# Two recurrent heads per group of small matmuls, the first weights on one queue, and other buffers: a change to a fused decoder layer

## The chip, the cores and the metric

One core of a Trainium2 chip runs the whole kernel. The metric is device time in microseconds (us) of one execution. The kernel before took 729.4 us as the median of three runs (727.81 to 729.68). One more execution was profiled; it took 726.6 us.

Names used: PE is TensorE (matmuls), PEld its weight loads, DVE is VectorE, ACT is ScalarE, POOL is GpSimd, SP is SyncE, which only issues DMAs here. SBUF is the working memory with 128 partitions, PSUM the memory that matmuls write.

## The reference

One layer of a decoder: 512 positions, model width 1024, everything in float32. Three groups of heads read the same normalised input; their outputs are joined and projected, and a feed-forward network follows.

```
h     = rmsnorm(x, norm_mix)
proj  = h @ w_in          # c_q, c_kv, k_rope, hq, hf, hi, hg, mq
y_mla = mla_group(...)    # 4 heads of causal attention from low-rank q and kv
y_hg  = hgrn2_group(hq, hf, hi, hg, ...)
y_mem = mem_group(mq, rmsnorm(mem), ...)   # 4 heads into 256 memory tokens
x     = x + concat(rmsnorm(y_mla), y_hg, rmsnorm(y_mem)) @ w_out
h2    = rmsnorm(x, norm_ffn)
x     = x + (silu(h2 @ w_gate) * (h2 @ w_up)) @ w_down
```

The recurrent group (hgrn2, four heads of width 128) is what the change is mostly about. With a forget gate f per position and feature, q = silu(hq)/sqrt(128), k = 1 - f, v = hi, the output at t is the sum over s <= t of (sum over features of q[t] k[s] f[s+1]...f[t]) v[s]. It is then normalised per head and gated with silu(hg).

## The kernel before, in words

**Order of the work.** The kernel is not issued in the order in which it is written. A recorder collects every operation, with its reads and writes, a class (0 is most urgent, 2 is filling work) and a price from a formula (`price`, L184). A planner (`run`, L241) then simulates the five engines and writes out one fixed order for each: at each step an engine takes what can start first, and among what is ready the lowest class, then the earliest in the program. Several operations may go to one of two or three engines. Buffers are named by a tag with a fixed count (`BUFS`, L426); an operation that needs a new buffer of a tag is held until one is free, and the planner plans with that. Nearly every instruction is therefore issued on L382; the groups of small matmuls that are recorded as one operation ("tiles") are issued on L379. In the profile a tile is called by its tag: tm<-in_xT is a load of the input into a buffer of tag "tm".

**Matmuls.** A float32 product is made of three fp32r matmuls. Each operand is split into a high part (a cast on ACT: wh, xh, hd, pth, mx) and a low part (a subtraction on DVE: wl, xl, ptl, mx). Products accumulate in PSUM: "mm" (three banks), "at" (three), "tr" (two).

**The start.** Weights of the first query and forget projections of the recurrent heads come in five loads (`EARLY`, L396): two from ACT's queue, three from SP's, between the eight loads of the input. The eight gains of the first norm come in a small load of their own on ACT's queue. Seven matmuls of 128 columns on a tile of ones (`WARM`, L395) run while PE waits. For each of eight chunks ACT makes the scaled high part, DVE the low part, and later the squares for the norm are summed in "td" buffers.

**Recurrent heads.** `hg_in` (L685) projects and gates a head: q, k and the running decay. `hg_levels` (L744) makes the scores of one head without ever dividing by a decay. It goes through sub-block sizes m = 1, 2, 4, ... 128. At each level the scores between the halves of every block of 2m are a matmul of q and k, and then q's upper halves and k's lower halves are multiplied by the decay of the other half (DVE, 256 elements a row each), and the decays are combined in pairs. For m up to 16 the scores lie within 32 x 32 squares of the diagonal: 16 small float32 matmuls (128 rows, 32 columns of weights, 32 moving) give all of them into one PSUM tile, and a predicated copy (DVE) takes those of this level into tile "cc". One more such group comes ahead of the levels, for the diagonal itself. For m = 32 there are 8 pieces, for m = 64 four matmuls of 64 x 64, for m = 128 and the two halves full matmuls. A float32 matmul shows as two instructions, so a group of 16 pieces has 32. The levels of one head keep a "p" buffer for the scores and a "p" buffer for the combined decays; there are two. `hg_out` (L812) multiplies scores with values and normalises, `hg_final` (L822) gates and splits the result into xh and xl.

**Column sums.** `colsum` (L534) sums squares over partitions: 16 small matmuls with a tile of ones, per tile of squares. It serves the norms and the four query heads of each attention, one call a head.

**The rest.** Memory tokens are loaded in four tiles of tag "td", scaled and split into "mx", and their squares summed. Low-rank projections, query and key projections, the causal attention (softmax in "p" buffers), the memory attention, the output projection in two passes (recurrent and causal parts first, in this order, then the memory part) and the feed-forward part follow. Projections that only need the input's split parts (xh, xl) are filling work of class 2.

Of the kernel before, what the change touches and what calls it, by code (L numbers as in the profile page):

```python
# [45 lines left out]
class Recorder:  # L46
# [137 lines left out]
    def price(self, o, outs, ins):  # L184
# [210 lines left out]
WARM = 7  # L395
EARLY = {0: (1, "p", "scalar"), 1: (2, "p", "scalar"), 3: (2, "tc", "sync"), 5: (2, "tc", "sync"), 7: (1, "tc", "sync")}  # L396
# [10 lines left out]
def body(ctx, tc, t):  # L407
# [14 lines left out]
    def nm(p):  # L422
# [5 lines left out]
        "pth": 2, "ptl": 2, "qr": 1, "p": 2, "mx": 8, "cc": 2, "sm": 12, "sd": 8, "mm": 3, "at": 3, "tr": 2,  # L428
# [27 lines left out]


# [7 lines left out]
    with rec.first(0):  # L465
        A.dma_start(out=sm[:, 0:8], in_=t["sm"][:, 0:8])
# [67 lines left out]
    def colsum(sq, nblk):  # L534

        o = ps_ts()
        T.tiles(o[:, 0:2 * nblk], lhsT=sq, rhs=ones, parts=[
            (o[g:g + 32, 2 * b:2 * b + 2], sq[:, b * P + g:b * P + g + 32], ones, b == 0, b == nblk - 1)
            for b in range(nblk) for g in range(0, P, 32)
        ])  # L540
        return o[:, 0:2 * nblk].rearrange("p (b two) -> p b two", two=2)[:, :, 0]
# [26 lines left out]
    def heads(ap):  # L568
        return ap.rearrange("p (h d) -> p h d", d=P)


    with rec.first(0):
# [3 lines left out]
        early = ([], [])  # L576
        for k in range(KD):
            if k in EARLY:
                n, tag, q = EARLY[k]
                w = sb(tag)[:, :2 * n * P]  # L580
                getattr(rec, q).dma_start(out=w, in_=t["we"][:, 2 * k * P:2 * (k + n) * P])
                pc = piece(w, 0, 2 * n * P)
# [6 lines left out]
            split(r, hi, lo, smc("g_mix", k))  # L589
# [154 lines left out]
    def hg_levels(q, k_, tot):  # L744
        A_ = sb("p", (P, NB, P))
        tt = sb("p")
        C = sb("cc", (P, NB, 32))
        toff = 0

        def scores():  # L750

            o = ps_at()[:, 0:NB * 32].rearrange("p (b t) -> p b t", t=32)
            T.tiles(o, lhsT=k_, rhs=q, parts=[
                (o[g:g + 32, b], k_[:, b * P + g:b * P + g + 32], q[:, b * P + g:b * P + g + 32], b == 0, b == NB - 1)
                for b in range(NB) for g in range(0, P, 32)
            ])
            return o

        o = scores()
        V.tensor_tensor(C, o, eye.unsqueeze(1).broadcast_to([P, NB, 32]), ALU.mult)  # L760
        G.memset(A_, 0.0)
        V.tensor_tensor(q, q, tot, ALU.mult)
        m = 1
        while m <= 128:
            if m <= 16:
                o = scores()
                V.copy_predicated(C, lmask[:, LEVELS.index(m), :].unsqueeze(1).broadcast_to([P, NB, 32]), o)
                if m == 16:
                    for g in range(0, P, 32):
                        A.copy(A_[g:g + 32, :, g:g + 32], C[g:g + 32])  # L770
            elif m == 32:
                o = heads(ps_at())[:, :, :32]
                T.tiles(o, lhsT=k_, rhs=q, parts=[
                    (o[i:i + 32, b], k_[:, b * P + i:b * P + i + 32], q[:, b * P + i + 32:b * P + i + 64], b == 0, b == NB - 1)
                    for b in range(NB) for i in (0, 64)
                ])
                for i in (0, 64):
                    A.copy(A_[i:i + 32, :, i + 32:i + 64], o[i:i + 32])
            elif m == 64:
                o = heads(ps_at())[:64, :, :64]  # L780
                for b in range(NB):
                    T.matmul(o[:, b], lhsT=k_[:, b * P:b * P + 64], rhs=q[:, b * P + 64:(b + 1) * P], start=b == 0, stop=b == NB - 1, skip_group_check=True)
                A.copy(A_[:64, :, 64:], o)
            else:
                pts = [new_pt(2), new_pt(4)]
                for g, pt in enumerate(pts):
                    for x in pt:
                        G.memset(f(x)[:, 4 * g + 2, :], 0.0)
                o = ps_at()
                for i, s in enumerate((0, 2)):  # L790
                    T.matmul(o[:, i * P:(i + 1) * P], lhsT=k_[:, s * P:(s + 1) * P], rhs=q[:, (s + 1) * P:(s + 2) * P], start=i == 0, stop=i == 1, skip_group_check=True)
                for i in range(2):
                    split(o[:, i * P:(i + 1) * P], pts[i][0][:, 4 * i + 1, :], pts[i][1][:, 4 * i + 1, :])
            n = S // (2 * m)
            tv = tot.rearrange("p (n two) -> p n two", two=2)
# [661 lines left out]
```

## Time and profile before

| | before |
|---|---|
| median of three runs | 729.4 us (727.81 to 729.68) |
| profiled execution | 726.6 us |
| its span, first to last instruction | 724.7 us |
| PE busy | 704.3 us (97%) |
| DVE busy | 563.0 us (78%) |
| ACT busy | 382.6 us (53%) |
| groups' instructions in the recurrent heads (at<-tm,tm on L379) | 832 |

The page and the views give, for a group of instructions, out<-in by the program's tags, shapes, the count, busy time, the mean of one in ns, and the idle time of the engine before them with what ended it. "Busy" of PE counts pipelined matmuls from their start to a modelled end, so two matmuls in a row overlap: the distance between two starts is what a matmul costs PE.

### The profile page before, as it was taken

The page shows a single profiled execution, that of the slowest core. Times are in us where ns is not written, and L with a number is a line of the kernel's source. Part 1 is how long each engine was busy: PE and PEld are TensorE (multiplying, and loading weights), DVE is VectorE, ACT ScalarE, POOL GpSimd, SP SyncE. Part 2 cuts the span into 40 slices and gives each one's busy share as a digit, 9 for nine tenths or more (in the row PEclk, how much of TensorE's full clock was granted, in tenths as well). Part 3 has the DMA queues.
Part 4 walks back from the last instruction along what each step waited for, and adds up shares of the span by engine and source line. Part 5 has one row for each costly group of instructions (what it writes and reads, how often), then busy time and mean ns, then how long its engine had stood idle before and what let it go on. Part 6 is the DMA issues. An engine that isn't in the chain of part 4 may idle for free.

```text
span 724.7 us, 13261 instructions
## 1 busy us (share of the span) xinstructions
PE 704.3 (97%) x4808; PEld 584.5 (81%) x4808; DVE 563.0 (78%) x1326; ACT 382.6 (53%) x726; POOL 93.0 (13%) x129
## 2 busy tenths in 40 slices
PE   7999999799999999899999999999999999999997
PEld 6888777678788887688686888888888899999886
DVE  6888889869988799897899979947548677538742
ACT  6743443437684487556477674635543355543420
POOL 0000000000000000000223323213202303410000
PEclk9999999999999999999999999999999999999999
DMA  8232122014621142121999999968958757942241
GB/s 277 76 107 70 60 89 74 24 38 140 195 97 34 55 137 92 49 59 44 263 266 214 256 215 226 229 151 220 219 146 165 180 135 172 219 110 41 66 131 72
DMA packets 47873, 98.07 MB, mean 135 GB/s; under 512 B 5568, under 2 KB 15680, under 8 KB 47808
## 3 DMA queue, kind: packets, MB, share of 16 engines
q1 hardware_dynamic: 33552, 73.75, 31.3%
q0 software_dynamic: 13824, 23.07, 20.3%
q8 instruction: 38, 0.62, 0.3%
q10 hardware_dynamic: 432, 0.40, 0.2%
q14 instruction: 27, 0.22, 0.1%
HBM read 95.11 MB, written 2.10 MB: 134 GB/s over the span
## 4 chain that ended last, share of the span: by engine, by line
PE 90%; DVE 6%; ACT 2%; issue 1%; DMA 0%; DVEq 0%; ACTq 0%
PE mm L382 47%; PE tr L382 21%; PE at L382 20%; PE at L379 1%; DVE wl L382 1%; PE tr L379 1%; DVE ptl L382 1%; DVE hd L382 1%; ACT L382 1%; DVE y L382 1%; DVE sm L382 0%; ACT p L382 0%; DMA tm<-in_xT 0%; DVE tm L382 0%; DVE tc L382 0%
## 5 line engine op out<-in xcount | busy, mean ns | idle before, releaser
L382 ACT CAST wh<-wr 128x512 fp32r<-128x512 f32 (+2 forms) x136 | 80.8, 598 | 113.7 <-PE mm L382 64.9
L382 DVE TENSOR_TENSOR wl<-wr,wh 128x512 fp32r<-128x512 f32 (+2 forms) x148 | 96.5, 657 | 33.2 <-issue 11.4
L382 PE MATMUL mm<-xh,wh 128*128 128x512 f32 x248 | 99.4, 406 | 5.5 <-ACT wh L382 3.2
L382 PE MATMUL mm<-xh,wl 128*128 128x512 f32 x248 | 100.2, 405 | 0.0
L382 PE MATMUL mm<-xl,wh 128*128 128x512 f32 x248 | 99.9, 404 | 0.2 <-DVE xl L382 0.2
L382 DVE TENSOR_TENSOR wl<-y,wh 128x512 fp32r<-128x512 f32 (+1 forms) x84 | 53.1, 637 | 42.2 <-PE tr L382 17.3
L382 ACT CAST wh<-y 128x512 fp32r<-128x512 f32 (+1 forms) x83 | 48.2, 582 | 66.5 <-PE at L382 34.2
L382 DVE TENSOR_TENSOR wl<-mx,wh 128x512 fp32r<-128x512 f32 (+1 forms) x72 | 45.6, 642 | 27.6 <-PE tr L382 14.8
L382 PE MATMUL mm<-wh,hd 128*128 128x512 f32 (+2 forms) x188 | 64.0, 366 | 0.7 <-ACT wh L382 0.7
L382 ACT CAST wh<-mx 128x512 fp32r<-128x512 f32 (+1 forms) x65 | 37.8, 584 | 40.9 <-PE at L382 22.1
L382 PEld LDWEIGHTS mm<-xh,wh 128*128 128x128 f32 x248 | 47.1, 191 | 14.5 <-ACT wh L382 3.6
L382 PEld LDWEIGHTS mm<-xl,wh 128*128 128x128 f32 x248 | 47.5, 191 | 8.7 <-DVE xl L382 0.7
L382 PEld LDWEIGHTS mm<-xh,wl 128*128 128x128 f32 x248 | 47.2, 190 | 8.4
L382 PE MATMUL at<-wh,hd 128*128 128x512 f32 (+1 forms) x132 | 49.7, 377 | 0.0
L382 POOL DMA_DIRECT2D y<-in_wu x36 | 32.5, 943 | 96.9 <-DVE wl L382 80.7
L382 PE MATMUL tr<-xl,wh 128*128 128x512 f32 x112 | 43.8, 391 | 0.0
L382 PE MATMUL tr<-xh,wl 128*128 128x512 f32 x112 | 43.7, 390 | 0.0
L382 PE MATMUL tr<-xh,wh 128*128 128x512 f32 x112 | 43.7, 390 | 0.0
L382 PEld LDWEIGHTS mm<-wh,hd 128*128 128x128 f32 x188 | 34.6, 188 | 5.8 <-ACT wh L382 1.1
L382 PE MATMUL mm<-wl,hd 128*128 128x512 f32 (+2 forms) x100 | 37.0, 370 | 0.2 <-DVE wl L382 0.2
L382 POOL MEMSET p<- 128x128 f32 (+1 forms) x12 | 3.7, 312 | 258.1 <-PE tr L382 116.8
L382 PE MATMUL mm<-wh,v 128*128 128x512 f32 (+1 forms) x96 | 36.1, 376 | 0.6 <-ACT v L382 0.6
(371 smaller groups left out, 1750.5 us busy)
## 6 DMA issues: line engine op xcount, KB each, us to landing
wr<-in_wf SPq DMA_DIRECT2D x19, 512.0 KB, 3.4
wr<-in_wd SPq DMA_DIRECT2D x16, 512.0 KB, 5.2
mx<-in_wg SPq DMA_DIRECT2D x24, 256.0 KB, 5.6
mx<-in_wu SPq DMA_DIRECT2D x24, 256.0 KB, 4.8
y<-in_wu POOLq DMA_DIRECT2D x24, 256.0 KB, 6.0
tm<-in_xT SPq DMA_DIRECT2D x16, 256.0 KB, 3.6
wr<-in_wt SPq DMA_DIRECT2D x8, 512.0 KB, 4.1
wr<-in_wo SPq DMA_DIRECT2D x8, 512.0 KB, 3.5
```

The source lines that it names most:

```text
L379: r = self.nc.tensor.matmul(get(a), lhsT=get(b), rhs=get(c), start=first, stop=last, skip_group_check=True)
L382: r = getattr(getattr(self.nc, o.eng), o.name)(*[get(a) for a in o.args], **{k: get(a) for k, a in o.kw.items()})
```

## The change

- `hg_levels` takes a list of two heads and goes through the levels with both. A group of small matmuls holds the pieces of both heads: 64 instructions at m = 2 to 16, 32 at m = 32, 16 of 64 x 64. The group for the diagonal and the one for m = 1 become one with 128, for which q times its decay goes to a new buffer of tag "y". One DVE operation then takes the scores of both heads. The combined decays are written in place, so the second "p" buffer holds the other head's scores. The level m = 128 moves into `hg_out`.
- `colsums` sums two tiles of squares in one group, for the query heads of both attentions.
- The five first weight loads are all on ACT's queue, ahead of everything else; the first also brings the eight gains. The constant pi/2 is made on ACT, right behind them, instead of on DVE. The warm-up is 12 matmuls of 512 columns.
- Homes: memory tokens load into "y" instead of "td"; the recurrent heads' split outputs go to "mx" instead of xh and xl, and those of the causal attention to xh and xl instead of "mx".
- The planner's price of a group of small matmuls has another formula.

```
-                return 180 + 64 * len(o.kw["parts"]) / len({self._rng(p[0])[2] for p in o.kw["parts"]})
+                return 310 + 1.81 * sum(max(35, self._free(p[2])) for p in o.kw["parts"]) / len({self._rng(p[0])[2] for p in o.kw["parts"]})
...
-WARM = 7
-EARLY = {0: (1, "p", "scalar"), 1: (2, "p", "scalar"), 3: (2, "tc", "sync"), 5: (2, "tc", "sync"), 7: (1, "tc", "sync")}
+WARM = 12
+EARLY = {0: (1, "p"), 1: (2, "p"), 3: (2, "tc"), 5: (2, "tc"), 7: (1, "tc")}
...
-        "pth": 2, "ptl": 2, "qr": 1, "p": 2, "mx": 8, "cc": 2, "sm": 12, "sd": 8, "mm": 3, "at": 3, "tr": 2,
+        "pth": 2, "ptl": 2, "qr": 1, "p": 2, "mx": 8, "cc": 1, "sm": 12, "sd": 8, "mm": 3, "at": 3, "tr": 2,
...
-    with rec.first(0):
-        A.dma_start(out=sm[:, 0:8], in_=t["sm"][:, 0:8])
...
-            T.matmul(o[:, 0:P], lhsT=ones_r, rhs=ones_r, start=True, stop=True)
+            T.matmul(heads(o), lhsT=ones_r, rhs=ones_r.unsqueeze(1).broadcast_to([P, NB, P]), start=True, stop=True)
...
-    V.memset(hpi, float(np.pi / 2))
...
+    def colsums(sqs, nblk=NB):
+        o = ps_ts()[:, 0:2 * nblk * len(sqs)]
+        ks = [(i, b) for i in range(len(sqs)) for b in range(nblk)]
+        v = o.rearrange("p (i b two) -> p i b two", two=2, b=nblk)
+        T.tiles(o, ones, *sqs, parts=[
+            (v[g:g + 32, i, b], sqs[i][:, b * P + g:b * P + g + 32], ones, (i, b) == ks[0], (i, b) == ks[-1])
+            for i, b in ks for g in range(0, P, 32)
         ])
+        return v[..., 0]
...
+        for k, (n, tag) in EARLY.items():
+            w = ws[k] = sb(tag)[:, :2 * n * P + 8 * (k == 0)]
+            A.dma_start(out=w, in_=t["we"][:, 2 * k * P + 8 * (k > 0):2 * (k + n) * P + 8])
+        gain = ws[0][:, 2 * P:]
+
+        A.mul(hpi, ones[:, 0:1], float(np.pi / 2))
...
-            split(r, hi, lo, smc("g_mix", k))
+            split(r, hi, lo, gain[:, k:k + 1])
...
-    def hg_levels(q, k_, tot):
+    def hg_levels(hs):
+
+        N2 = range(len(hs))
+        As = [sb("p", (P, NB, P)) for i in N2]
+        C = sb("cc", (P, len(hs), NB, 32))
+        old, hs = hs, [(sb("y"), k_, tot) for q, k_, tot in hs]
...
+            T.tiles(o, *[x for i, h in all_ for x in h[:2]], parts=[
+                (o[g:g + 32, i, b], h[1][:, b * P + g:b * P + g + 32], h[0][:, b * P + g:b * P + g + 32], (i, b) == (all_[0][0], 0), (i, b) == (all_[-1][0], NB - 1))
+                for i, h in all_ for b, g in ps_
             ])
...
+        def put(o, m):
+            V.copy_predicated(C, lmask[:, LEVELS.index(m), :].unsqueeze(1).unsqueeze(1).broadcast_to([P, len(hs), NB, 32]), o)
+
+        for (q, _, tot), (q1, _, _) in zip(old, hs):
+            V.tensor_tensor(q1, q, tot, ALU.mult)
...
+            if m == 1:
+                o, o1 = scores([old, hs])
+                V.tensor_tensor(C, o, eye.unsqueeze(1).unsqueeze(1).broadcast_to([P, len(hs), NB, 32]), ALU.mult)
+                put(o1, 1)
+            elif m <= 16:
+                put(scores([hs])[0], m)
...
+            hs = [(q, k_, step_up(q, k_, tot, m)) for q, k_, tot in hs]
             m *= 2
+        return [(A_,) + h for A_, h in zip(As, hs)]
...
+        if m < 128:
+            V.tensor_tensor(tot[:, 0:n], tv[:, :, 0], tv[:, :, 1], ALU.mult)
+        return tot
...
-        hi = sb("xh", dt=F32R)
-        lo = sb("xl", dt=F32R)
+        hi = sb("mx", dt=F32R)
+        lo = sb("mx", dt=F32R)
         split(y, hi, lo)
         mix[4 + h] = (hi, lo)
...
+    for h, st in enumerate(hg_levels(qkf)):
+        yh.append(hg_out(h, *st))
+    qkf = [hg_in(2), hg_in(3)]
+    for h, st in enumerate(hg_levels(qkf)):
+        yh.append(hg_out(2 + h, *st))
...
-            r = sb("td", (P, 2, NM))
+            r = sb("y", (P, 2, NM))
             DMA.dma_start(out=r, in_=t["memT"][:, k * S:(k + 1) * S].rearrange("p (a b) -> p a b", a=2))
...
+            sq.append(sumsq([o]))
+        if h % 2:
+            V.tensor_copy(sq_n[:, :, h - 1:h + 1].rearrange("p b h -> p h b"), colsums(sq[-2:]))
...
-    group_norm(ym, 0, "g_mla", ("mx", "mx"))
+    group_norm(ym, 0, "g_mla", ("xh", "xl"))
```

More of the change, by code (lines that the diff above doesn't have):

```diff
@@ L534, in colsum @@
     def colsum(sq, nblk):
[L536 to L539, printed above, removed]
+        return colsums([sq], nblk)[:, 0]
+    def colsums(sqs, nblk=NB):
[5 more added lines that the diff above has]
+            for i, b in ks for g in range(0, P, 32)
         ])
-        return o[:, 0:2 * nblk].rearrange("p (b two) -> p b two", two=2)[:, :, 0]
+        return v[..., 0]
     def spread(r):
@@ L777, in hg_levels @@
[L777 to L783, printed above, removed]
-            else:
[L785 to L793, printed above, removed]
@@ new lines, in hg_out @@
+    def hg_out(h, A_, q, k_, tot):
+        pts = [new_pt(2), new_pt(4)]
+        for g, pt in enumerate(pts):
+            for x in pt:
+                G.memset(f(x)[:, 4 * g + 2, :], 0.0)
+        o = ps_at()
+        for i, s in enumerate((0, 2)):
+            T.matmul(o[:, i * P:(i + 1) * P], lhsT=k_[:, s * P:(s + 1) * P], rhs=q[:, (s + 1) * P:(s + 2) * P], start=i == 0, stop=i == 1, skip_group_check=True)
+        for i in range(2):
+            split(o[:, i * P:(i + 1) * P], pts[i][0][:, 4 * i + 1, :], pts[i][1][:, 4 * i + 1, :])
+        step_up(q, k_, tot, 128)
@@ L918, in body @@
     w = [piece(r, 0, 512) for r in wuq]
+    sq = []
     for h in range(4):
```

97 lines of the change are left out of this document (44 added, 53 removed).

## Prediction

> **What bounds the kernel now.** I read the page first: the engines' shares and the chain that ended last.
>
> ```profile
> span 724.7 us, 13261 instructions
> ...
> PE 704.3 (97%) x4808; PEld 584.5 (81%) x4808; DVE 563.0 (78%) x1326; ACT 382.6 (53%) x726; POOL 93.0 (13%) x129
> ...
> PE 90%; DVE 6%; ACT 2%; issue 1%; DMA 0%; DVEq 0%; ACTq 0%
> ```
>
> PE is busy for 97% of the span and is 90% of the chain. An edit pays only if it takes time out of PE's own stream or fills one of PE's few holes. The view of windows (window, length, then PE, PEld, DVE, ACT and POOL busy, granted clock, DMA share, GB/s) shows the holes around the recurrent heads and the attention behind them.
>
> ```profile
> 34.00:127.00 93.00, 92.58 (x1303) 75.73 (x1303) 80.86 (x250) 39.32 (x80) 3.32 (x12) 1.00 0.25 79
> 127.00:138.00 11.00, 7.06 (x135) 4.80 (x132) 9.07 (x23) 5.33 (x12) 0.00 (x0) 0.84 0.12 37
> 138.00:201.00 63.00, 62.59 (x500) 50.30 (x498) 53.72 (x177) 36.59 (x73) 0.20 (x1) 1.00 0.34 110
> 201.00:275.00 74.00, 74.00 (x525) 61.59 (x524) 63.70 (x167) 46.76 (x95) 1.81 (x7) 1.00 0.26 82
> 275.00:298.00 23.00, 18.94 (x126) 14.95 (x124) 19.71 (x52) 13.63 (x28) 0.20 (x1) 0.93 0.22 69
> ```
>
> PE is full from 34 to 127 and from 138 to 275 us. DVE stands next behind it, at 87% and 85% of the two stretches before 201. The holes are 127 to 138 (3.9 us idle, granted clock 0.84) and 275 to 298 (4.1 us idle, at the end of the causal attention). So up to about 275 us PE's time is what a saving is counted in.
>
> **Fewer groups of small matmuls.** PE's own order of time around one group of score pieces (start, duration), then the row that groups all of them (count, busy us, mean ns of one, idle before):
>
> ```profile
> 93.85 0.40 PE L382 MATMUL mm<-xh,wl 128*128 128x512 f32 x1
> 94.17 0.46 PE L379 MATMUL at<-tm,tm 128*32 128x32 f32 x32
> 94.56 0.50 PE L382 MATMUL mm<-xh,wh 128*128 128x512 f32 x1
> 94.90 0.40 PE L382 MATMUL mm<-xl,wh 128*128 128x512 f32 x1
> 95.13 0.39 PE L382 MATMUL mm<-xh,wl 128*128 128x512 f32 x1
> ```
>
> ```profile
> L379 PE MATMUL at<-tm,tm 128*32 128x32 f32 x832 | 13.0, 199 | 2.9 <-DVE tm L382 2.9
> ```
>
> Two large matmuls in a row start 0.23 us apart (94.90 to 95.13). From 93.85 to 94.90 there are two of these and one group: 1.05 - 2 x 0.23 = 0.59 us for the group. Inside the group, from the first small start to the last, lie 0.46 - 0.20 = 0.26 us (its busy time less the mean of one); those are the 32 instructions of its 16 pieces. The other 0.33 us is a fixed price, paid at the two ends where PE goes from large to small and back. Merging two groups saves 0.33 us and keeps the 0.26.
>
> How many fixed prices go: the 832 instructions are 24 groups of 32 (six a head) and 4 groups of 16. With two heads together a pair has one group for the first two score sets, four for sub-blocks 2 to 16, and one for 32: six, twelve in all instead of 28. The 64-wide step goes from four groups to two; I give it the same price. That is 18 prices x 0.33 = 5.9 us. The query projections' column sums, groups of 16 pieces too and priced alike, go twice from four to two. The first two groups saved lie before 201, where PE is full: 2 x 0.33 = 0.6 us. The other two stand under the causal attention, whose own end leaves PE idle at 275 to 298; I count them at nothing (0.6 us if that hole were gone).
>
> The bounds: nothing, if all of the 0.59 went with the number of small matmuls, and 18 x 0.59 = 10.6 us, if a second head's pieces came free. The small starts 8 ns apart exclude the first, and the 0.26 us excludes the second.
>
> The Trainium skill speaks against the saving: "TensorEngine Tiling (Array Packing)", section Performance Considerations, gives about 60 cycles to each matmul, which I estimate at 25 ns with the 2.4 GHz of "TensorE: Matmul & The Clock Gate". Taken one after the other, 32 of them would be 0.8 us with nothing fixed, merging would save nothing, and the sum below would be 4.0 instead of 10.5. The trace disagrees: 32 starts lie in 0.26 us.
>
> On DVE the pairing halves a number of instructions too:
>
> ```profile
> L382 DVE COPY_PREDICATED cc<-lmask,at 128x128 f32<-128x128 uint8 x20 | 5.9, 297 | 2.0 <-PE at L379 2.0
> ...
> L382 DVE TENSOR_TENSOR tm<-tm,p 128x256 f32<-128x256 f32 x56 | 22.4, 417 | 0.0
> ```
>
> 20 x 0.297 becomes 10 of twice the width, priced like the 256-wide row at 0.42: 5.9 to 4.2, so 1.7 us less of DVE. The scaling of the queries, now into a buffer of its own, is the same work. The running product written in place waits for the two multiplications before it, on the same engine, in order.
>
> **The new wait: two heads in step.** A merged group waits for the later of two heads, and on PE the large matmuls queued behind it wait too. What covers it is other ready work; which order results is the planner's. In its favour: no head now holds a "p" buffer from its first level for running products, so the second pair need not wait for the first pair's scores to be read out. DVE, at 87%, is the engine that could make PE wait. Bounds: 2 us gained (its 1.7 saved) to 3 us lost. I take 1.0 us lost.
>
> **The hole at 127 us.** PE's order of time there, then the timing of tile td:
>
> ```profile
> 127.53 0.46 PE L379 MATMUL at<-tm,tm 128*32 128x32 f32 x32
> 130.40 0.46 PE L379 MATMUL at<-tm,tm 128*32 128x32 f32 x32 [2.41 <-DVE tm L382]
> 131.94 0.50 PE L382 MATMUL mm<-xh,wh 128*128 128x512 f32 x1 [1.08 <-ACT td L382]
> ...
> 133.68 0.80 PE L382 MATMUL mm<-xh,wl 128*128 128x512 f32 x1
> ...
> 135.98 0.63 PE L382 MATMUL mm<-xl,wh 128*128 128x512 f32 x1
> ```
>
> ```profile
> L382 SPq DMA_DIRECT2D td<-in_memT x4: 327/328/423, 95.4 to 123.5; - x4
> ...
> L382 ACT ACTIVATE td<-mm x3: 597/597/597, 131.3 to 134.7; 128x512 f32<-128x512 f32 x3
> ```
>
> At 127.5 PE has only one head's levels left and waits 2.41 us for DVE's step of them. It has no large matmul to put between, because the next projection waits for ACT's square of an earlier one (td<-mm, 131.3 us), which has to read the PSUM bank before it comes free. That square waits for one of three td buffers, and these are held by the memory tokens (td<-in_memT, the last at 123.5 us) and their sum. In the change the tokens load into y, so td is free and the square can run when the projection ends. The hole costs 11.0 - 7.06 = 3.9 us idle, and five matmuls from 133.68 to 135.98 take 2.30 us where 5 x 0.23 = 1.15 is usual: together 5.1 us. I take 4.0 of it; bounds 0 (another buffer is next) and 5.1.
>
> On the half rate the Trainium skill ("TensorE: Matmul & The Clock Gate", Part 1, the table of states) says that the clock falls after an idle window of about 3.4 us. Here the longest idle was 2.41 us and the clock fell. By that rule the hole would cost 3.9 us, and the term would be about 3.1.
>
> **The start.** Two stretches of PE's windows (warm-up, first real matmuls), and the rows of ACT and PE that lead to the second:
>
> ```profile
> 1.20:3.10 1.90, 1.76 (x7) 1.57 (x7) 0.00 (x0) 0.00 (x0) 0.10 (x1) 1.00 0.58 135
> ...
> 6.10:10.45 4.35, 4.31 (x10) 3.32 (x11) 3.93 (x7) 3.64 (x7) 0.53 (x1) 1.00 1.04 375
> ```
>
> ```profile
> 3.78 1.28 ACT L382 ACT_TABLE_LOAD   x1 [3.78 <-DMA tm<-in_xT]
> ...
> 6.14 1.22 PE L382 MATMUL mm<-xh,wh 128*128 128x512 f32 x2 [3.17 <-ACT wh L382]
> ```
>
> PE's first 10 real matmuls take 4.31 us, where 10 x 0.23 = 2.3 would do: as if it had started at full rate at 8.1 (6.1 + 2.0). Twelve warm-up matmuls of 512 columns instead of seven of 128 keep PE busy up to them: 12 x 0.43 (half rate, 4.31/10) = 5.2 us from 1.2 to 6.4 at most, less if the rate rises on the way. I expect the real ones at full rate then.
>
> Against it stands ACT's queue, which now issues five weight loads before its first arithmetic. SP's queue at the start, its wait, and the time to landing of a first weight load show what that meets:
>
> ```profile
> 0.74 1.33 SPq L382 DMA_DIRECT2D tm<-in_xT  x3
> 2.12 0.43 SPq L382 DMA_DIRECT2D tc<-in_we  x1
> 2.59 1.64 SPq L382 DMA_DIRECT2D tm<-in_xT  x2
> ```
>
> ```profile
> SPq L382 <- DMA smv<-in_sm: 0.9, 1, 0.9
> ```
>
> ```profile
> p<-in_we ACTq DMA_DIRECT2D x1, 128.0 KB, 3.7
> ```
>
> With ACT's three loads SP's fifth is the eighth of all. Its sixth, the ninth, waits 0.9 us until the first of all, the gain vector from ACT's queue, has landed, at 2.59 + 0.43 + 0.9 = 3.9. So eight are in flight at a time. In the change loads alternate between the two queues, and the ninth is ACT's fifth. It waits for the first weight load, which lands at 0.74 + 3.7 = 4.4, or at 3.9 if it is as quick as the gain vector was. Behind this wait are queued the issue (0.43), the table load (1.28), the one-column constant (I take 0.2, under the 0.297 of a 128-wide DVE row above) and the two splits (PE started 1.08 us after the table load's end): 6.9 to 7.4. I take 7.1 at full rate: 8.1 - 7.1 = 1.0 us gained. Bounds: 2.5 (no wait: five issues end at about 3.0, the table load at 4.3, the first split starts when its data is there at 4.4, PE at 5.6) and -1.0 (PE at 7.1 and cold again, worth 2.0). DVE's clearing of that constant goes, at nothing.
>
> **Homes without a price.** The splits of the recurrent heads' outputs move from xh, xl to mx, and the causal attention's from mx to xh, xl. The former can run earlier (mx is free after the memory projections), the latter need the input's split halves read out by the last gate projection. PE's idle time at 275 to 298 says that no such projection was left by then, so they are free before the attention ends. If that cover went, the output projection would start on the recurrent heads' part, which is first in its order. I count 0.
>
> **The sum.** 5.9 + 0.6 + 4.0 + 1.0 - 1.0 = 10.5 us. The profiled execution took 726.6 us (span 724.7 and 1.9 around it), so 716.1. It lies 2.8 under the median of the runs, 729.4, so the median goes to 718.9, forecast 719.
>
> **The rivals.** Savings turn to idle: the causal attention's chain, not PE, ends at 298, and if it starts no earlier, PE only runs out of other work sooner. Against it: PE is full for 63 us before it, with a chain that feeds on PE's own projections. Only start and noise would be left, a gain of 0 to 2: about 728.5, no change.
>
> Paired squares hold td: the first head's squares now stay in one of the three td buffers until the second head's projection is squared, while gates want two more. This is the same shortage as at 127 us, and it decides where a bank's square has to wait while PE has no other ready work. A hole of 5.1 us each: two give back 10.2 of the 10.5 (729, no change), three (two in the query projections, one in the memory queries) give 10.5 - 15.3 = -4.8: 734, slower. Against it: paired projections follow one another, and with little else in td.
>
> The hole at 275 goes too: the recurrent heads' outputs leave y and are ready sooner, and the memory attention, which needs y, fills in. Its 4.1 us more give 715.
>
> The loads do not do what they are moved for: ACT is held as above and PE is cold, -1.0 instead of 1.0: 721, inside the forecast's own range of 715 to 725.
>
> The price goes with the count: 0.59 us over 32 instructions is 18 ns each, nothing is fixed, and merging saves neither the 5.9 nor the 0.6: a gain of 4.0, 725.4. Against it: the starts 8 ns apart. This is what the rule on the cost of each matmul in the Trainium skill ("TensorEngine Tiling (Array Packing)", Performance Considerations) would do here.
>
> **How the numbers follow.** Forecast 0.61, the better case 0.15, idle instead of gain 0.12, td slower 0.09, a price by count 0.03. A difference under 0.3% (2.2 us) can't be told from none. Faster is 0.61 + 0.15 + 0.03 and 0.01 of the idle case, 0.80; same 0.11; slower 0.09. The range, 712 to 729, takes in all cases but the slower one, and the largest saving of the start and the hole (1.5 + 1.1 more than taken, with the better case).
>
> **What would show it.** L379's score instructions stay 832 in 12 clusters of 32, 64 and 128, each a fixed 0.33 us; no PE wait of 1 us or more for ACT td near 120 us; PE at 0.23 us spacing from its first real matmul, at about 7 us; PE's time from 34 to 201 shorter by some 9 us. Wrong, if that stretch keeps its length with PE idle in it, or the clusters cost 1.2 us for two heads.

## The result and the profile after

The change took the median from 729.08 us (727.81 to 729.68) to 712.05 us (711.61 to 712.68): 0.9769 of before, 95% interval 0.9752 to 0.9786, 17.0 us less. The profiled execution took 712.43 us. The first lines of the page after answer to those of before:

```profile
span 710.7 us, 13219 instructions
...
PE 698.4 (98%) x4813; PEld 582.9 (82%) x4813; DVE 558.4 (79%) x1305; ACT 384.2 (54%) x731; POOL 94.0 (13%) x129
...
PE 93%; DVE 4%; ACT 2%; DMA 1%; issue 0%; DVEq 0%; ACTq 0%
```

PE is busy for 5.9 us less, of a span that is 14.0 us shorter; the other 8 us were idle time. The windows show where. The stretches answer roughly to those of before, the later ones 8 to 14 us earlier (window, length, PE, PEld, DVE, ACT, POOL, granted clock, DMA share, GB/s):

```profile
34.00:118.00 84.00, 83.66 (x1225) 71.70 (x1224) 72.90 (x201) 41.46 (x82) 2.05 (x7) 1.00 0.27 89
118.00:130.00 12.00, 11.68 (x169) 9.08 (x170) 10.61 (x41) 5.29 (x14) 0.00 (x0) 1.00 0.12 36
130.00:190.00 60.00, 59.73 (x541) 48.68 (x541) 55.31 (x186) 37.42 (x78) 0.71 (x4) 1.00 0.36 115
190.00:262.00 72.00, 72.00 (x518) 60.12 (x517) 63.20 (x171) 42.58 (x90) 2.39 (x8) 1.00 0.25 78
262.00:284.00 22.00, 20.19 (x137) 15.79 (x136) 21.11 (x53) 14.87 (x28) 1.19 (x2) 1.00 0.31 96
```

The hole of 127 to 138 us is closed: 0.3 us idle in 12, at a granted clock of 1.00 instead of 0.84. The hole at the end of the causal attention is 1.8 us instead of 4.1, also at full clock. From the view of PE's waits (total, times, longest):

```profile
PE mm L382 <- ACT xh L382: 4.8, 3, 2.2
...
PE mm L379 <- DVE td L382: 0.6, 2, 0.3
```

The three for ACT's xh are the start (1.3), the attention's end (1.2) and the end of the memory attention (2.2). None is left for ACT's td.

**Which part came where.** For a finer measure I counted PE's large matmuls at the distance of their starts when PE is full (0.227 us for 512 columns, 0.173 for 384, 0.147 for 320, 0.120 for 256; some 625 us in all) and compared the times at which two kernels have done the same amount. "Lead" is how much earlier than in the shown profile of before that is, at six of its times:

| kernel | 15 us | 118 | 201 | 302 | 360 | 700 | last block of third head | third head |
|---|---|---|---|---|---|---|---|---|
| before | 0 | 0 | 0 | 0 | 0 | 0 | 4.89 | 25.4 |
| after | -0.6 | 5.7 | 10.4 | 14.8 | 12.2 | 14.1 | 2.85 | 20.2 |
| e12 before again | -0.9 | -1.0 | -1.3 | -2.0 | -1.9 | -1.9 | | |
| e1 homes old | -0.3 | 6.0 | 10.7 | 15.2 | 13.4 | 13.8 | 2.85 | 20.2 |
| e2 tokens in td | -0.2 | 5.0 | 2.9 | 1.7 | -3.0 | -1.6 | 4.89 | 24.3 |
| e3 before, tokens in y | 0.2 | -2.7 | 2.1 | 0.9 | 1.0 | 0.8 | 4.89 | 25.4 |
| e4 one head a group | -0.2 | -0.8 | 4.6 | 4.6 | -0.8 | 0.4 | 4.89 | 24.3 |
| e5 table load early | -0.7 | 5.7 | 10.5 | 15.0 | 13.1 | 13.8 | 2.85 | 20.2 |
| e6 old warm-up | -0.7 | 5.8 | 10.5 | 15.0 | 12.9 | 14.8 | 2.85 | 20.2 |
| e7 single sums | -0.2 | 6.2 | 10.1 | 9.1 | 9.1 | 8.8 | 6.07 | 24.0 |
| e8 old price | 0.0 | 7.1 | 11.6 | 12.1 | 7.6 | 9.1 | 4.91 | 24.4 |
| e9 before, tanh | -0.5 | -0.5 | -0.8 | 1.6 | 0.2 | -0.3 | 4.36 | 22.8 |
| e10 after, tanh | -0.3 | 6.0 | 10.6 | 16.0 | 16.4 | 15.0 | 2.83 | 20.0 |
| e11 e8 with tanh | -0.3 | 6.8 | 11.2 | 11.2 | 11.3 | 11.2 | 4.36 | 22.6 |

The last two columns belong to the end of the causal attention: the time from the exponential of the third query block to that of the last one in its third head, and the length of that head, from the end of the second head's last value matmul to the end of its own. The fourth head, not in the table, takes 22.8 us in before and 24.1 in after, so the two heads together are 3.9 us shorter and not 5.2. The shown execution of before lies some 2 us below its median, so a lead reads that much smaller than a difference of medians.

So after has lost 0.6 us at 15 us, gained 10.4 by 201, 4.4 more by 302 at the attention's end, lost 2.6 of it by 360 and got 1.9 back.

**A merged group.** PE's order of time around one group of two heads in after (start, duration), and the rows of all groups of score pieces:

```profile
44.06 0.31 PE L382 MATMUL mm<-wl,xh 128*128 128x320 f32 x1
44.30 0.76 PE L379 MATMUL at<-y,tm 128*32 128x32 f32 x64
44.99 0.41 PE L382 MATMUL mm<-wh,xl 128*128 128x320 f32 x1
45.24 0.31 PE L382 MATMUL mm<-wh,xh 128*128 128x320 f32 x1
45.39 0.31 PE L382 MATMUL mm<-wl,xh 128*128 128x320 f32 x1
```

```profile
L379 PE MATMUL at<-y,tm 128*32 128x32 f32 x704 | 9.5, 199 | 0.0
...
L379 PE MATMUL at<-y,tm 128*64 128x64 f32 x32 | 2.5, 226 | 0.1
...
L379 PE MATMUL at<-tm,tm 128*32 128x32 f32 x128 | 1.9, 198 | 0.0
```

From 44.06 to 45.24 there are two matmuls of 320 columns (45.39 - 45.24 = 0.15 each) and one group of 64: 1.18 - 0.30 = 0.88 us. Inside it, 0.76 - 0.20 = 0.56. The fixed part is 0.32, as it was 0.33 around 32 instructions. The score instructions are 704 + 128 = 832, as before. Their distance depends on how many groups of 32 columns the pieces go to in turn: at m = 2 to 16 it is four groups, and 64 instructions lie in 0.56 us (9 ns apart); at m = 32 it is two, and the 32 instructions at 62.57 us last 0.70 us, 0.50 from the first start to the last (16 ns apart). So each column group takes some 32 to 36 ns a matmul in both, an estimate from these two rows.

**The start.** ACT (its queue's issues are ACTq) and PE in after:

```profile
0.74 0.89 ACTq L382 DMA_DIRECT2D p<-in_we  x2
1.66 3.21 ACTq L382 DMA_DIRECT2D tc<-in_we  x3
4.90 1.28 ACT L382 ACT_TABLE_LOAD   x1 [4.90 <-DMA p<-in_we]
```

```profile
1.22 4.84 PE L382 MATMUL tr<-ones_r 128*128 128x512 f32 x12 [1.22 <-DVE ones_r L382]
7.37 0.73 PE L382 MATMUL mm<-xh,wh 128*128 128x512 f32 x2 [1.31 <-ACT xh L382]
...
8.49 0.40 PE L382 MATMUL mm<-xh,wl 128*128 128x512 f32 x1
8.73 0.39 PE L382 MATMUL mm<-xl,wh 128*128 128x512 f32 x1
```

The fifth load holds ACT until 4.87, the table load follows, and PE starts at 7.37 at full rate (8.49 to 8.73). All of this is as forecast, and yet the lead at 15 us is -0.6. At full rate PE has to wait for the splits: its weight loads wait 0.49, 0.43 and 0.54 us for DVE's low part (xl) at 8.15, 9.81 and 12.94 us, while ACT works on without a wait. From 7.37 to 15 us PE loses 1.4 us that way, counted as the distance of its starts above 0.227 us; in before it lost 2.1 to the half rate from its start at 6.14 on.

### The profile page after: what moved, and what is told of

The parts are those of the page before. It is cut to its first block, busy times and chain, and to the rows that moved or that the text cites. A ratio compares the mean times of both kernels' runs of the same rounds, so it can differ in the third digit from the quotient of the medians.

```text
span 710.7 us, 13219 instructions
## 1 busy us (share of the span) xinstructions
PE 698.4 (98%) x4813; PEld 582.9 (82%) x4813; DVE 558.4 (79%) x1305; ACT 384.2 (54%) x731; POOL 94.0 (13%) x129
## 4 chain that ended last, share of the span: by engine, by line
PE 93%; DVE 4%; ACT 2%; DMA 1%; issue 0%; DVEq 0%; ACTq 0%
PE mm L382 49%; PE tr L382 21%; PE at L382 21%; PE at L379 1%; PE tr L379 1%; DVE wl L382 1%; DMA p<-in_we 1%; DVE ptl L382 0%; DVE y L382 0%; DVE xl L382 0%; ACT L382 0%; DVE td L382 0%; PE mm L379 0%; DVE qr L382 0%; ACT wh L382 0%
## 5 line engine op out<-in xcount | busy, mean ns | idle before, releaser
L382 DVE TENSOR_TENSOR wl<-wr,wh 128x512 fp32r<-128x512 f32 (+2 forms) x148 | 96.8, 659 | 33.2 <-PE mm L382 11.6
L382 PE MATMUL mm<-xh,wh 128*128 128x512 f32 x248 | 97.4, 398 | 4.8 <-ACT xh L382 4.8
L382 ACT CAST wh<-y 128x512 fp32r<-128x512 f32 (+1 forms) x83 | 48.2, 582 | 68.5 <-PE at L382 35.5
L382 PEld LDWEIGHTS mm<-xh,wh 128*128 128x128 f32 x248 | 46.6, 189 | 13.8 <-ACT xh L382 5.7
L382 PEld LDWEIGHTS mm<-xl,wh 128*128 128x128 f32 x248 | 47.1, 190 | 11.2 <-DVE xl L382 2.5
L382 PE MATMUL at<-wh,v 128*128 128x512 f32 (+1 forms) x96 | 35.9, 374 | 0.0
```

The lines of the kernel that those rows point to most:

```text
L382: r = getattr(getattr(self.nc, o.eng), o.name)(*[get(a) for a in o.args], **{k: get(a) for k, a in o.kw.items()})
```

## The experiments

The medians of before beside the experiments were 728.69 (e1 to e4; 726.56 to 730.87), 728.24 (e5 to e8) and 728.52 us (e9 to e12). The first theory was the prediction's, term by term; its rival was that the tokens' and outputs' homes make up what it counted too small. Later runs asked what decides the attention's end.

**e1_homes_old** (after, only the homes of the outputs back):

```
-        hi = sb("mx", dt=F32R)
-        lo = sb("mx", dt=F32R)
+        hi = sb("xh", dt=F32R)
+        lo = sb("xl", dt=F32R)
...
-    group_norm(ym, 0, "g_mla", ("xh", "xl"))
+    group_norm(ym, 0, "g_mla", ("mx", "mx"))
```

> The changed kernel with the two old homes for the split outputs: recurrent heads in xh and xl, causal attention in mx. The changed kernel left 2.3 us of stalls around the end of the causal attention where before had 5.7, and gained 4.5 us there on the same PE work. Theory H: the new homes did it, since the recurrent heads' outputs no longer wait for the input's split halves to be read; then this run loses 3 to 5 us against the changed kernel (715 to 717) and shows the hole at the end of the causal attention again. Theory P: the attention's chain itself ended earlier against PE's other work, for other reasons; then this run stays within 1.5 us of the changed kernel (711 to 713.5).

Measured: 712.88 us (712.69 to 715.05), ratio 0.9795 [0.9777, 0.9813], at most a microsecond from after. The third head still takes 20.2 us, and the lead at 302 is 15.2. These homes are worth nothing that can be told, and are not what closed the hole at the attention's end.

**e2_tokens_td** (after, memory tokens loaded into td again; shown) and **e3_before_tokens_y** (before, with the opposite edit alone, y for td):

```
-            r = sb("y", (P, 2, NM))
+            r = sb("td", (P, 2, NM))
```

> The changed kernel with the memory tokens loaded into td again. Theory T (the hole at 127 us came from td buffers held by the tokens): a PE wait for a square into td or a hole of 1 us or more comes back between 95 and 145 us, and the time rises by 2 to 5 us (714 to 717). Rival: pairing the heads removed the hole, by ending the recurrent part sooner; then nothing comes back and the time stays within 1.5 us (711 to 713.5).

> The kernel before with one edit: memory tokens load into y instead of td. Theory T: the hole at 127 to 138 us closes, 4 to 5 us faster than before (724 to 725). Rival (pairing removed the hole): heads still go one after another, the hole stays, within 1.5 us of before (728 to 730).

e2: 727.82 us (726.73 to 728.31), ratio 0.999 [0.998, 0.9999]: 15.8 us slower than after. Its window and PE's order of time at the place of the hole:

```profile
118.00:130.00 12.00, 7.02 (x132) 5.49 (x119) 10.75 (x33) 5.66 (x13) 0.00 (x0) 0.72 0.10 36
```

```profile
117.67 0.76 PE L379 MATMUL at<-y,tm 128*32 128x32 f32 x64
122.08 1.30 PE L379 MATMUL at<-y,tm 128*32 128x32 f32 x32 [3.64 <-DVE tm L382]
124.70 0.79 PE L382 MATMUL mm<-xh,wh 128*128 128x512 f32 x1 [1.32 <-ACT td L382]
```

The same two waits as in before, on DVE's step and on ACT's square in td, each longer (3.64 for 2.41, 1.32 for 1.08); I read the difference so that both heads of the pair now stand at this step and neither has other levels to offer. At 201 us 7.5 us are missing (2.9 for 10.4); 5.6 more go at the attention's end and 2.6 after it, most of them at the end of the memory attention.

e3: 725.84 us (725.58 to 727.74), ratio 0.997 [0.996, 0.998], 2.9 us faster than before. The hole at 127 closes: its lead rises by 4.8 us from 118 to 201. But it had lost 2.7 before that, most of it near 26 us, where PE now waits for the first norm's spread:

```profile
27.56 0.62 PE L382 MATMUL tr<-cst,rx 128*128 128x128 f32 x4 [0.82 <-issue]
28.86 0.42 PE L382 MATMUL tr<-wh,xh 128*128 128x320 f32 x1 [0.68 <-ACT RX L382]
```

So the tokens' home is shown to be the hole's cause, alone and with the pairing, and the pairing needs it: the tokens' home is worth 4.8 us at this place in before and 7.5 in after.

**e4_one_head** (after, groups of one head; the first two score sets and the query sums stay merged):

```
-    for h, st in enumerate(hg_levels(qkf)):
-        yh.append(hg_out(h, *st))
+    for h in range(2):
+        yh.append(hg_out(h, *hg_levels(qkf[h:h + 1])[0]))
```

and the same for heads 2 and 3.

> The changed kernel with the levels of one head at a time (the group for the diagonal and the one for m = 1 stay one): 24 groups of score pieces instead of 12 and four 64-wide steps instead of two, 14 fixed prices of 0.33 us more. Theory T (the fixed price is PE's and PE is the bound): 4.6 us slower than the changed kernel, 716 to 717.5. Rival (the price goes with the number of small matmuls): no difference, 711 to 713. Rival (two heads in step cost PE more than they save): faster than 711.

Measured: 726.22 us (724.98 to 727.49), ratio 0.9968 [0.9955, 0.998], 14 us slower than after. Of these only 5.8 lie in the recurrent heads' own stretch (4.6 for 10.4 at 201): 14 more groups at 0.41 us each, for the 4.6 us expected at 0.33. PE's waits between 15 and 195 us are 0.6 longer (1.2 for 0.6), which is half of the difference. The other 8 come later, 4.4 at the attention's end and most of the rest at the end of the memory attention.

**e7_sums_single** (after, each head's column sums by themselves; the cut is the memory attention's, the causal one's is alike):

```
-            if h % 2:
-                V.tensor_copy(vq[:, :, h - 1:h + 1].rearrange("p b h -> p h b"), colsums(sq[-2:]))
+            V.tensor_copy(vq[:, :, h], colsum(sq[-1], NB))
```

> The changed kernel with column sums of the query heads one head at a time again, both attentions: four groups more. Theory: two fixed prices of 0.33 us ahead of the causal attention, 0.7 us slower, and two under it that may cost nothing: 712.5 to 713.4. Rival (pairs of squares hold td buffers): no slower or faster, 710 to 712.

Measured: 717.64 us (717.35 to 718.64), ratio 0.9849 [0.9828, 0.987], 5.6 us slower than after. At 201 us only 0.3 of it is there. By 302 us 5.4 more are lost: the third head takes 24.0 us. The edit's own part there is two more groups, which lie under the second and third heads (205 to 235 us) and cost 0.7 us at the price above; the rest comes from the order.

**e8_price_old** (after, with the planner's old price of small matmuls; the computation is the same, but the planner's order differs, and with it the engine of some casts, copies and scalings):

```
-                return 310 + 1.81 * sum(max(35, self._free(p[2])) for p in o.kw["parts"]) / ...
+                return 180 + 64 * len(o.kw["parts"]) / ...
```

> The changed kernel planned with the old price of a group of small matmuls (the computation is the same, only the planner's order can differ). Theory: the orders differ little, within 1.5 us of the changed kernel (710.5 to 713.5). Rival: the surplus over the forecast came from a better plan; then 715 or more.

Measured: 718.49 us (717.54 to 718.78), ratio 0.9856 [0.9835, 0.9876], 6.4 us slower than after. It is 1.2 us ahead of after at 201 us, and then loses 3.9 at the attention's end and 1.9 more by 360. The plan alone decides these two places.

**What differs at the attention's end.** The third head's last two exponentials on ACT, in before and in after:

```profile
253.29 0.67 ACT L382 ACTIVATE p<-at,sm,rq 128x384 f32<-128x384 f32 x1
...
254.06 1.28 ACT L382 ACT_TABLE_LOAD   x1
256.88 1.28 ACT L382 ACT_TABLE_LOAD   x1
258.18 0.78 ACT L382 ACTIVATE p<-at,sm,rq 128x512 f32<-128x512 f32 x1
```

```profile
240.03 0.67 ACT L382 ACTIVATE p<-at,sm,rq 128x384 f32<-128x384 f32 x1 [0.95 <-PE tr L382]
...
242.88 0.77 ACT L382 ACTIVATE p<-at,sm,rq 128x512 f32<-128x512 f32 x1
...
243.76 1.28 ACT L382 ACT_TABLE_LOAD   x1
245.06 0.63 ACT L382 ACTIVATE td<-td 128x512 f32<-128x512 f32 x1
```

And the maximum of the last block (sm<-at) and the first operation of a recurrent head's gate (td<-mm,RX) on DVE, in before and in after:

```profile
253.40 0.68 DVE L382 TENSOR_TENSOR td<-mm,RX 128x512 f32<-128x512 f32 x1
255.31 0.69 DVE L382 TENSOR_REDUCE sm<-at 128x1 f32<-128x512 f32 x1
```

```profile
241.75 0.68 DVE L382 TENSOR_REDUCE sm<-at 128x1 f32<-128x512 f32 x1
...
244.01 0.68 DVE L382 TENSOR_TENSOR td<-mm,RX 128x512 f32<-128x512 f32 x1
```

In before a gate becomes ready while the last block's softmax is under way. Its operations are of class 0, the softmax's of class 1, so the planner puts them in between on both engines, and on ACT the gate's sigmoid brings two table loads, its own and that back to the exponential. From exponential to exponential that is 4.89 us instead of 2.85. Every one of the seven versions in which the gate's operation stands ahead of the maximum (before, e2, e3, e4, e8, e9, e11) needs 4.4 or more there and 22.6 to 25.4 us for the head; the five in which it stands behind (after, e1, e5, e6, e10) need 2.8 to 2.9 and about 20. In e7 the maximum is first, but the sigmoid and its two loads come ahead of the exponential: 6.07.

**e9_before_tanh, e10_after_tanh, e11_price_old_tanh**: before, after and e8 with the recurrent heads' four late gates by a tanh, since sigmoid(z) is (1 + tanh(z/2))/2. The Trainium skill ("ScalarE: Activation LUTs", section Table sets: the hidden batching unit) lists tanh in the same set as exp, so that no load would stand between them.

```
-    def gated(i):
+    def gated(i, fn=AF.Sigmoid, scale=1.0):
...
-            A.activation(s_, z, AF.Sigmoid)
+            A.activation(s_, z, fn, scale=scale)
...
-            z, s_ = gated(13 + h)
-        V.tensor_tensor(z, z, s_, ALU.mult)
-        V.tensor_tensor(y, y, z, ALU.mult)
+            z, s_ = gated(13 + h, AF.Tanh, 0.5)
+        V.scalar_tensor_tensor(z, s_, 1.0, z, ALU.add, ALU.mult)
+        V.scalar_tensor_tensor(y, z, 0.5, y, ALU.mult, ALU.mult)
```

> The kernel before with the four late gates of the recurrent heads written with a hyperbolic tangent, z times (1 + tanh(z/2)) / 2, instead of a sigmoid; nothing else differs. Before, ACT's function table was loaded three times inside the third head of the causal attention (at 254.1, 256.9 and 260.9 us) and that head took 25.4 us against 20.2 in the changed kernel, which loads it once there. Theory S (these loads stand between the head's exponentials and make the hole at 275 to 298): if the tangent needs no load beside the exponential, the third head takes 20 to 22 us, and the time falls by 4 to 7 us, to 722 to 725. Rival (the order of the projections under the attention makes the difference, the loads only follow it): within 2 us of before.

> The changed kernel with the same four gates by tangent. Theory S: the changed kernel already has its third head without the extra loads and keeps a stall of 2.3 us at the attention's end and five loads in the last head; 1 to 4 us faster than the changed kernel, 708 to 711. Rival (no share of the loads): within 1 us of 712.

> The changed kernel with the old price and the four gates by tangent. With the old price alone the same work on PE was reached 1.3 to 3.3 us earlier than in the changed kernel up to 260 us, and 5 us were lost at the end of the causal attention, where the third head had three table loads. Theory S: the loss goes, 709 to 713, 5 us or more under the old price alone (718.5). Rival (the plan itself is worse): 716 or more.

The table loads of after and of e10 (count, busy us, mean ns, idle before):

```profile
L382 ACT ACT_TABLE_LOAD x14 | 18.0, 1283 | 8.2 <-DMA p<-in_we 4.9 <-DVE sm L382 3.1
```

```profile
L382 ACT ACT_TABLE_LOAD x8 | 10.3, 1283 | 4.7 <-DMA p<-in_we 4.6
```

The trace agrees with the Trainium skill: 14 loads become 8.

e9 took 727.22 us (725.8 to 731.1), ratio 0.9995 [0.9978, 1.0011]: no gain that can be told, where 722 to 725 was expected. At the attention's end the theory holds in part: the third head takes 22.8 us, where 20 to 22 was expected, but the third and fourth together take 44.0 us, as in after (44.3; before 48.2), and the lead rises by 2.4 from 201 to 302. By 360 most of that is lost again (0.2), and it ends at -0.3.

e10 took 711.46 us (711.3 to 711.74), ratio 0.9765 [0.9749, 0.9781]: the fastest kernel of the study, by 0.6 us, which is within the intervals. Its lead rises by 5.4 from 201 to 302, 1.0 more than that of after.

e11 took 715.93 us (715.34 to 717.28), ratio 0.9829 [0.9814, 0.9843]: 2.6 us faster than e8, and between the theory (709 to 713) and its rival (716 or more). But nothing of it comes at the attention's end. The third head takes 22.6 us instead of 24.4, the fourth 25.0 instead of 23.0, and from 201 to 302 the lead stays at 11.2 where that of e8 rises by 0.5. The gain lies between 302 and 360, where e8 loses 4.5 and e11 nothing.

So the loads are a part of the loss at the attention's end in before, and in the order of e8 taking them out saves nothing there. The gate's place in the order costs without them too: 4.36 us between the two exponentials in e9 and e11, with loads 4.89 and 4.91 (before and e8), in after 2.85. Why the planner puts the gate ahead in one version and behind in the next wasn't tried by itself and stays open.

**The end of the memory attention.** In e8 (and e2, e4) PE's queue has one more operation ahead of the small transposes, and waits 3.4 to 3.5 us for it; in after it waits 2.25 behind them (before: 1.25, e11: 1.26). e8, then after:

```profile
341.21 0.76 PE L382 MATMUL tr<-td,ones_r 128*128 128x512 f32 x1 [3.40 <-DVE sm L382]
```

```profile
335.12 0.62 PE L382 MATMUL tr<-cst,sm 128*128 128x128 f32 x4
337.99 0.96 PE L382 MATMUL mm<-xh,wh 128*128 128x512 f32 x3 [2.25 <-ACT xh L382]
```

**e5_const_early** (after, the one-column constant, and with it the table load, ahead of the fifth weight load) and **e6_warm_old** (after, the old warm-up):

```
         for k, (n, tag) in EARLY.items():
+            if k == 7:
+                A.mul(hpi, ones[:, 0:1], float(np.pi / 2))
...
-        A.mul(hpi, ones[:, 0:1], float(np.pi / 2))
```

```
-WARM = 12
+WARM = 7
...
-            T.matmul(heads(o), lhsT=ones_r, rhs=ones_r.unsqueeze(1).broadcast_to([P, NB, P]), start=True, stop=True)
+            T.matmul(o[:, 0:P], lhsT=ones_r, rhs=ones_r, start=True, stop=True)
```

> The changed kernel with the one-column constant (and so the table load) on ACT ahead of the fifth weight load instead of behind it. In the changed kernel the table load stood behind the wait for the first weight load and began at 4.90 us; PE's first real matmul came at 7.37. Theory: the wait of the fifth load no longer holds the table load, which begins at about 2.6 and ends by 4; the first split then follows the fifth issue at about 4.9, PE starts at 5.9 to 6.2, and the gain is 1.0 to 1.4 us (710.5 to 711). Rival: the start is bound by the loads' arrival and by ACT's and DVE's splitting, and PE waits later instead; gain under 0.4 us.

> The changed kernel with the old warm-up (seven matmuls of 128 columns). Theory: PE is cold at its first real matmuls, 0.43 us apart for some 4 us, 1.5 to 2 us slower (713.5 to 714). Rival: the first matmuls are bound by arriving data, so the half rate is hidden; within 0.5 us.

e5: 712.63 us (712.42 to 712.9), ratio 0.9778 [0.9758, 0.9797], the same as after. Its rows on ACT:

```profile
2.63 1.28 ACT L382 ACT_TABLE_LOAD   x1 [2.63 <-issue]
...
6.33 0.34 ACTq L382 DMA_DIRECT2D tc<-in_we  x1
6.71 0.40 ACT L382 CAST wh<-p 128x256 fp32r<-128x256 f32 x1 [2.58 <-DMA p<-in_we]
```

The table load is early, but the fifth load still stands ahead of the first cast in ACT's queue, and now it issues at 6.33, after three more issues of SP's queue (4.03, 4.40 and 6.08). The wait was moved, not removed, so the run doesn't tell whether the data would have let PE start sooner.

e6: 712.5 us (711.77 to 713.45), ratio 0.978 [0.9756, 0.9805], the same again. With the old warm-up the first matmuls run at half rate:

```profile
6.93 1.22 PE L382 MATMUL mm<-xh,wh 128*128 128x512 f32 x2 [3.96 <-ACT xh L382]
...
8.81 0.63 PE L382 MATMUL mm<-xl,wh 128*128 128x512 f32 x1
9.24 0.63 PE L382 MATMUL mm<-xh,wl 128*128 128x512 f32 x1
```

At 15 us it has done as much as after, -0.7 and -0.6. This flatters it: its fifth load was issued by 4.44 us, that of after by 4.87, so PE started 0.44 us sooner. e2 and e7 start at 6.98 with the long warm-up and stand at -0.2. So the longer warm-up is worth some 0.5 us at equal loads, an estimate from single profiles, where 1.5 to 2 were expected; the medians can't tell it. Most of the full rate is lost again because PE is then paced by the splits.

**e12_before_again** (before, unchanged, one execution):

> The kernel before once more, for its profile. Its profiled execution (726.6 us) lay at the low end of its runs (726.6 to 730.9). Theory C: after PE's holes its rate comes back at moments that differ from run to run, so a run near the median differs from the shown profile in stretches right behind the holes (start, 127 to 138, 282 to 300, 350). Rival: the difference is spread evenly.

It took 728.53 us, 1.9 more than the shown profile, and its lead says where: 0.9 at the start, 0.3 around 127 us and 0.7 around 300. The window of the hole at 127:

```profile
127.00:138.00 11.00, 7.67 (x126) 5.27 (x112) 9.21 (x26) 5.39 (x12) 0.00 (x0) 0.70 0.12 37
```

The granted clock was 0.70 there, for 0.84 in the shown one. At both holes the granted clock is down to 0.50 for a while: in the shown profile for 3.4 us (133.2 to 136.6 and 293.6 to 297.0), in e12 for 6.8 (131.5 to 138.3 and 295.3 to 302.1). Executions of the same kernel differ at the start and in these stretches. Behind its start after has one such stretch, 339.7 to 343.1 us, and e10 none. The four times of after spread over 1.1 us, the four of before beside them over 1.9, and the 24 beside e1 to e4 over 4.3.

## Why the prediction was right, and where its size was not

The forecast was faster, 719.0 us; it is 712.05, at the very edge of the range of 712 to 729. The steps, in the order of the sum:

- **Fewer groups, 5.9, and the column sums, 0.6.** Held. A group of 64 costs 0.88 us where the rule "same fixed part, twice the inside" gives 0.33 + 2 x 0.26 = 0.85. Undoing 14 of the 18 prices costs 5.8 us at 201 (0.41 each, with some waiting in it), undoing the sums 0.3. The rival in which the price goes with the count gave 2 x 0.59 = 1.18 for that group; it falls. The Trainium skill's "TensorEngine Tiling (Array Packing)" says two things here. Its 60 cycles a matmul (Performance Considerations) don't fit if the matmuls are taken one after another, as in the prediction: starts 8 to 9 ns apart against the 25 estimated there. Counted for each of the four column groups, some 32 to 36 ns, they are not contradicted. Its Key Properties, that a change of the tiling mode drains TensorE, fit the 0.32 us for the two changes around a group, though no run shows a drain as such.
- **Two heads in step, -1.0.** No run measures it by itself. From 15 to 201 us the lead rises by 11.0; without 5.9 and 0.6 that leaves 4.5 for the hole and the pairing together, where 3.0 was forecast. With the 4.8 that the hole is worth in e3 the pairing would cost 0.3, an estimate. It stays open.
- **The hole at 127, 4.0.** Held in kind and in size. The lead rises by 4.7 us from 118 to 201, a stretch that also holds two of the 18 prices and the sums, and e2 and e3 show the tokens' home to be the cause. Not foreseen was that pairing without it makes the hole worse (7.5 instead of 4.8), so that most of what the pairing saves would be lost again.
- **Paired squares hold td.** Didn't come: no wait of PE for ACT's td is left, and 0.6 us for DVE's.
- **The start, 1.0.** The mechanism came as described (fifth load held, table load behind it, first matmul at 7.37, inside the 6.9 to 7.4 worked out, and at full rate), and the gain did not: -0.6 against the shown before, +0.3 against e12. The eight profiles with the start of after (e5 and e6 left out) lie at -0.6 to 0.0, the four with that of before at -0.9 to 0.2, and both average -0.3: no gain. The step that failed is the assumption that PE, once at full rate, stays fed: it loses 1.4 us by 15 us to waits for the splits, which was put at nothing.
- **Up to 201 us**, then, 10.4 us against the 10.5 of the sum. That this fits so closely is luck: the start fell short by 1.6, the other terms gave 11.0 for 9.5.
- **Savings turn to idle.** Didn't come: the lead of 10.4 at 201 us is 14.1 at the end.
- **"I count 0" for the homes** was right for them (e1). What failed is what hung on it: that the hole at 275 stays as it is. The lead rose by 4.4 us there, 2.6 were lost at the end of the memory attention and 1.9 came back: 3.7 net. The better case (715) had the hole going, at 0.15, but for another reason, recurrent outputs ready sooner; with the homes back the hole stays closed. What goes with it is the gate that stands inside the third head's last softmax in before and behind it in after. That order and length go together in twelve versions, and that the plan alone can make the difference (e8), is shown. Which edit makes the planner's order fall well in after isn't: taking back the tokens' home, the pairing, the paired sums or the price each spoils it. The forecast knew nothing of this order, so these 3.7 us are luck: e7 and e8, within 1.2 us of after at 201, ended at 717.64 and 718.49 us.
- **From the profile to the median.** I carried the 2.8 us by which the profiled execution lay below its median over to after. There the profiled one lies 0.4 above it. That is 3.2 us of the 6.9 by which the forecast was too high; the attention's end and what follows it are the other 3.7. e12, near before's median, lost its 1.9 us at the start and at the two holes that the change closes or shortens.

## What to carry to other kernels

Split the price of a group of small instructions into its two ends and its inside before pricing a merge, and check in the same stretch which waits of the merged parts have no other work left to cover them: here the saving held only because a buffer tag was freed as well. Where a planner writes the order, edits worth a microsecond or nothing where they act (e7, e8) moved 5 us elsewhere, so a forecast's range should hold one reshuffle of each tight stretch, to both sides. And a profiled execution's distance to its median belongs to the stalls of that kernel; it doesn't carry over to one in which they are gone.

## What the runs showed of the hardware

- A group of 128 x 32 matmuls among full ones costs about 0.32 us beside its instructions, for 32 as for 64 of them. Its starts are 8 to 9 ns apart with four column groups in turn, 16 with two.
- A load that can't be issued yet holds everything behind it on its engine: the fifth issue ended at 4.87 us in after and, with the table load moved ahead, at 6.67 in e5, and ACT's first cast came behind it.
- An exponential and a tanh need no table load between them (14 loads became 8). A load takes 1.28 us and the next activation follows at once (243.76 to 245.06). The Trainium skill ("ScalarE: Activation LUTs", What ACT_TABLE_LOAD costs) gives about 1.28 us for it, which agrees, and 1.38 for a drain besides, which these rows don't show behind the load.
- At the hole of 127 us, with 2.41 us the longest single wait of PE, the granted clock fell to 0.50 for 3.4 us in before and for 6.8 in e12.
